# Where weight tiles lie against activations, modulo 512 bytes, in a two-layer encoder

## Chip, core and metric

The kernel runs on one core of a Trainium2 chip. The metric is the time of one execution on the device in microseconds (us); lower is better. Profiles are one execution each, taken by the hardware profiler. Engines are named PE (TensorE's matmuls), PEld (its weight loads), DVE (VectorE), ACT (ScalarE), POOL (GpSimd) and SP (SyncE, whose queue issues most loads).

## What is computed

Two encoder layers over 256 tokens of width 2,048, in float32. Layer 0 mixes tokens by 2-D neighbourhood attention with a position bias (12 heads), layer 1 by grouped-query attention with rotary positions (12 heads, 4 key heads). In both, 4 more heads attend to 256 memory tokens. The sum of all products with weights is what takes the time:

```python
for i in range(DEPTH):                       # 2
    n = rms_norm(h, attn_norm[i])
    z = n @ (a_w_in[j] if i % 2 == 0 else b_w_in[j])   # 2048 x 5120, 2048 x 3072
    ...                                      # attention of the layer's own heads
    km, vm = jnp.split(m @ w_mem_kv[i], 2, axis=-1)
    cross = memory_attention(...)
    h = h + jnp.concatenate([mix, cross], axis=-1) @ w_o[i]
    n = rms_norm(h, mlp_norm[i])
    h = h + jnp.square(jax.nn.relu(n @ w_up[i])) @ w_down[i]   # width 8192
return rms_norm(h, final_norm)
```

## The kernel before

Every weight chunk of 128 x 2048 float32 (1 MB) is loaded by SP, then taken apart into a high part in the reduced float32 format (`hi`, `uh`, `th`, ...; ScalarE, `split`, L301) and the rest as a low part (`lo`, `ul`, `tl`, ...; VectorE, L302). Activations are held in the same two parts. A product is then three matmuls: high x high, high x low, low x high. A half of a chunk is 128 x 1024, 4,096 bytes in each partition.

There are two sorts of product:

- *S products and up products* (`s_products`, L215; `u_products`, L690): the weight tile is the stationary operand, 128 x 128, and the activations (`memT`, `nT`, `hT`) stream past it, 256 columns. They write `ps_s` (memory keys, q and k of layer 0) and `ps_u` (the MLP's up projection).
- *M products and down products* (`m_products`, L202; the function at L804): the activations are stationary and the weights stream, 512 columns. They write `ps_m` and the seven sums `p1` to `p7` of a Strassen-like scheme, in which `a_s` holds the activations' combinations and `bh`, `bl`, `th`, `tl` the weights'.

The attention itself (`sc_ps` and `av`, L352 to L354 and L386 to L388) multiplies activations alone, 256 columns, in the same pattern of three.

The MLP runs as one long row: `up_grains` of a part and `down_grains` of the part before alternate; on TensorE about 48 up products (two halves of a chunk) stand before 21 down products. A list of grains (`run_all`) decides the program's order; loads, splits and products are issued some grains ahead of each other.

Tiles come from pools. A pool places its tiles one behind the other, so the start of a tile follows from the lengths of those before it. At four places the kernel before sets a start by hand: `MOVING_AT` (160 bytes) and `STILL_AT` (64 bytes) shift the used part of a half inside a tile that is 256 bytes longer than its content, and `wide(name, 480)` shifts `nT` by 480 bytes. Since such a tile is 4,352 bytes long, neighbouring buffers of one name differ by 256, modulo 512. The lines in question:

```python
def new_half(kind):
    s = slice(STILL_AT // 4, STILL_AT // 4 + HALF) if kind == "S" else slice(0, HALF)
    return tuple(at.ring.tile([P, HALF + 64], F32R, tag=n, bufs=4, name=n)[:, s] for n in ("hi", "lo"))
```

Of the kernel before, what the change touches and what calls it, by code (L numbers as in the profile page):

```python
# [10 lines left out]
F32 = mybir.dt.float32  # L11
F32R = mybir.dt.float32r
# [5 lines left out]
P = 128  # L18
# [16 lines left out]
HALF = CH // 2  # L35
# [3 lines left out]
STEPS = PK // 2  # L39
GUARD = 3  # L40

MOVING_AT = 160

STILL_AT = 64
MASKED = -1e30


# [27 lines left out]
def encoder_kernel(ctx: ExitStack, tc: tile.TileContext, t: dict, out: bass.AP):  # L75
# [4 lines left out]
    def opened(name, side="left", space=None, bufs=1):  # L80
        kw = {"space": space} if space else {}
        manager = tc.tile_pool(name=name, bufs=bufs, side=side, reuse_waits="tile", **kw)
        pools[name] = manager, manager.__enter__()
        return pools[name][1]
# [14 lines left out]
    def open_sums():  # L99
        at.acc = opened("ps_acc", space=bass.MemoryType.PSUM, bufs=4)  # L100
        at.att = opened("ps_att", space=bass.MemoryType.PSUM, bufs=4)

    def open_ring():
        at.ring = opened("ring")
        at.cat = opened("cat")

    def open_work():
        at.work = opened("work", side="right", bufs=2)
# [36 lines left out]
    def halves_of(w):  # L145

        tiles = {}

        def load():
            tiles["raw"] = loaded(w.src, "U")  # L150

        def prep_early(hf):
            tiles[hf] = half_of_side(tiles["raw"], hf, MOVING_AT)

        def prep(hf):
            if hf == 0:
                tiles["raw"] = at.ring.tile([P, CH], F32, tag="raw", bufs=3, name="raw")
                nc.sync.dma_start(tiles["raw"], w.src)
            tiles[hf] = new_half(w.kind)
            split(*tiles[hf], tiles["raw"][:, hf * HALF : (hf + 1) * HALF])  # L160

        def run(hf):
            if hf == 0:
                w.start(w)
            hi, lo = tiles.pop(hf)
            if w.kind == "S":
                s_products(w, hf * (KT // 2), KT // 2, hi, lo)
            else:
                for i in range(NT):
                    m_products(w, w.first + 2 * hf, 2, i, hi, lo, w.begins and hf == 0, w.last and hf == 1)  # L170

        def after():
            if w.last:
                w.done(w)
            if w.early == "last":
                to_work()

        if w.early:
            return [Grain(lambda: run(0), None, load, None, lambda: prep_early(0), SOON),
                    Grain(lambda: run(1), after, None, None, lambda: prep_early(1), SOON)]  # L180
        return [Grain(lambda: run(0), None, None, None, lambda: prep(0)),
                Grain(lambda: run(1), after, None, None, lambda: prep(1))]

    def new_half(kind):
        s = slice(STILL_AT // 4, STILL_AT // 4 + HALF) if kind == "S" else slice(0, HALF)
        return tuple(at.ring.tile([P, HALF + 64], F32R, tag=n, bufs=4, name=n)[:, s] for n in ("hi", "lo"))

    pin = tc.keep_in_program_order

# [338 lines left out]

    def x_norm(j):
        if j == 0:  # L530
            box["nT"] = wide("nT0", 480)
        for k in (2 * j, 2 * j + 1):
            split_pair(box["nT"], box["xT"][k // 8][:, k % 8, :], G_A0, k)

# [162 lines left out]
            nc.tensor.matmul(ps, hi[:, s], acts[:, k, SEQ:], start=False, stop=False)  # L697
            nc.tensor.matmul(ps, lo[:, s], acts[:, k, :SEQ], start=False, stop=k == KT - 1)  # L698

    def half_of_side(raw, hf, place=0):  # L700
        s = slice(place // 4, place // 4 + HALF)
        tiles = tuple(at.side.tile([P, HALF + 64], F32R, tag=n, bufs=2, name=n)[:, s] for n in ("uh", "ul"))
        box.setdefault("splits", []).append(split(*tiles, raw[:, hf * HALF : (hf + 1) * HALF]))
        return tiles

# [5 lines left out]
    def up_grains(layer, part, m):  # L711
        own = {}

        def load():
            own["raw"] = loaded(t[f"w_up{layer}"][part * PK + m], "U")

        def prep(hf):
            own[hf] = half_of_side(own["raw"], hf)

        def run(hf):  # L720
            if hf == 0:
                if part == 0:
                    own["ps"] = at.acc.tile([P, 512], F32, tag="acc", name="ps_u")[:, :SEQ]
                else:
                    if part == 1 and m == 0:
                        closed("ps_att", "ps_acc")
                        at.sums = opened("ps_sums", space=bass.MemoryType.PSUM)
                        box["ps"] = {}
                    own["ps"] = at.sums.tile([P, 512], F32, tag="up", name="ps_u")[:, :SEQ]
            u_products(own["ps"], hf * (KT // 2), KT // 2, *own.pop(hf))  # L730

        def after():
            if part == 0 and m == 0:
                closed("cat", "ring")
                at.mlp = opened("mlp")
                box["z"] = [at.mlp.tile([P, 4, 512], F32, tag=f"z{q}", name=f"z{q}") for q in range(2)]
                box["z_set"] = set()
            squared(layer, part, m, own["ps"])

        return [Grain(lambda: run(0), None, load, None, lambda: prep(0), SOON),  # L740
                Grain(lambda: run(1), after, None, None, lambda: prep(1), SOON)]
# [25 lines left out]
    def down_grains(layer, part, n, begins, ends):  # L767

        q, j = part % 2 ^ n // STEPS, n % STEPS
        own = {}  # L770

        def load():
            src = t[f"w_pair{layer}"][(part * 2 + q) * STEPS + j]
            own["b"] = at.side.tile([P, 3 * 512], F32, tag="b", bufs=2, name="b")
            nc.sync.dma_start(own["b"], src[:, : 3 * 512])
            own["t"] = at.side.tile([P, 4, 512], F32, tag="T", bufs=2, name="t")
            nc.sync.dma_start(own["t"][:, 0, :], src[:, 3 * 512 :])

        def behind(fn):

            return (lambda: past(fn, box["splits"][-4])) if part == 0 and n < 2 else fn

        def block(k):

            return own["b"][:, k * 512 : (k + 1) * 512]

        def pre():
            s = own["t"]
            nc.vector.tensor_tensor(s[:, 1, :], s[:, 0, :], block(0), op=ALU.add)  # L789
            nc.gpsimd.dma_start(s[:, 0, :], block(1), accum_op=ALU.add)  # L790

        def prep_first():
            own["first"] = tuple(at.mlp.tile([P, 3 * 512], F32R, tag=x, name=x) for x in ("bh", "bl"))
            split(*own["first"], own["b"])

        def prep_second():
            s = own["t"]
            nc.vector.tensor_tensor(s[:, 2, :], s[:, 1, :], block(1), op=ALU.add)
            nc.vector.tensor_tensor(s[:, 3, :], s[:, 2, :], block(2), op=ALU.add)
            own["second"] = tuple(at.mlp.tile([P, CH], F32R, tag=x, name=x) for x in ("th", "tl"))  # L800
            split(*own["second"], s.rearrange("p a b -> p (a b)"))

        def run(which, products):
            hi, lo = own.pop(which)  # L804
            a = box["a", part, j]
            for name, ai, bi in products:
                if begins:
                    box["ps"][name] = at.sums.tile([P, 512], F32, tag=name, name=name)
                ps, s = box["ps"][name], slice(bi * 512, (bi + 1) * 512)
                nc.tensor.matmul(ps, a[:, 0, ai, :], hi[:, s], start=begins, stop=False)  # L810
                nc.tensor.matmul(ps, a[:, 0, ai, :], lo[:, s], start=False, stop=False)  # L811
                nc.tensor.matmul(ps, a[:, 1, ai, :], hi[:, s], start=False, stop=ends)  # L812

        def after(products):
            if ends:
                for name, _, _ in products:
                    taken(q, name)

        def after_second():
            after(SECOND)  # L820
            if ends:
                box["z_set"].add(q)
            if ends and (part, n) in FOLDS:
                folded(q)

        return [Grain(lambda: run("first", FIRST), lambda: after(FIRST), load, behind(pre), behind(prep_first), SOON),
                Grain(lambda: run("second", SECOND), after_second, None, None, behind(prep_second), SOON)]

# [35 lines left out]
    def plain_grains(layer, nb):  # L864
# [8 lines left out]

        def prep(c, hf):
            if c == 0:
                own[c, hf] = half_of_side(own[0], hf, MOVING_AT)
            else:
                own[c, hf] = tuple(at.mlp.tile([P, HALF], F32R, tag="bt"[hf] + x, name=f"{x}_p") for x in "hl")
                split(*own[c, hf], own[1][:, hf * HALF : (hf + 1) * HALF])
# [59 lines left out]
    def down_done(layer, nb):  # L939
        def f(w):  # L940
# [5 lines left out]
                later(1, times_gf, nb)  # L946
                return
            if nb == 0:
                box["nT"] = wide("nT1", 480)
            later(1, transposed, box["nT"], lambda i, k: h[:, i, k * P : (k + 1) * P],  # L950
                  list(range(nb * 4, nb * 4 + 4)), G_A1)
            if nb == 3:
# [278 lines left out]
```

## Time and profile before

| | us |
|---|---|
| median of 3 runs (2051.68 to 2055.82) | 2052.95 |
| span of the profiled execution (its own time is not recorded apart; the median is 2.35 above the span) | 2050.6 |
| TensorE busy, 13,092 matmuls | 2028.0 |
| weight loads busy | 1835.2 |
| VectorE busy | 1657.1 |
| ScalarE busy | 1242.0 |
| GpSimd busy | 120.2 |

Busy time of TensorE is the union of its matmuls, from start to modelled end. Because they are pipelined, a matmul's listed duration is longer than its distance to the next one's start. That distance is read from the timeline, which has one row per matmul with its start.

### The profile page before, as it was taken

What the parts mean: (1) busy time and instruction counts of PE and PEld (TensorE: products, weight loads), DVE (VectorE), ACT (ScalarE), POOL (GpSimd) and SP (SyncE); (2) the same over time, 40 slices, a digit from 0 to 9 for tenths busy, and PEclk for the clock granted to TensorE, in tenths of its full rate; (3) what the DMA queues carried; (4) which work ended last, traced back from release to release, by engine and by line L of the source; (5) the groups of instructions that cost most, each with busy time, mean ns of one, the idle gap of its engine ahead of it and who ended that gap; (6) DMA issues with size and microseconds to landing.
All of it is one profiled execution on the core that took longest, in us unless ns stands there. A gap on an engine that the chain in (4) does not pass through costs nothing.

```text
span 2050.6 us, 32620 instructions
## 1 busy us (share of the span) xinstructions
PE 2028.0 (99%) x13092; PEld 1835.2 (89%) x13092; DVE 1657.1 (81%) x2025; ACT 1242.0 (61%) x1616; POOL 120.2 (6%) x144
## 2 busy tenths in 40 slices
PE   8999999999999999999999999999999999999998
PEld 7899999889999999999988888889999999999996
DVE  6766666558998999989896667657989999999896
ACT  6645454556666666666655557556666666666664
POOL 0000000000000000000000001000000000000000
PEclk9999999999999999999999999999999999999999
DMA  7755555727777777777765554537878787777773
GB/s 280 284 190 180 189 175 178 275 86 224 234 228 232 218 238 230 220 234 226 232 219 204 178 180 144 195 115 224 242 223 237 215 243 220 232 226 228 231 220 134
DMA packets 93431, 433.84 MB, mean 212 GB/s; under 512 B 10464, under 2 KB 12128, under 8 KB 60128
## 3 DMA queue, kind: packets, MB, share of 16 engines
q1 hardware_dynamic: 75888, 399.25, 57.7%
q0 software_dynamic: 16816, 31.46, 8.7%
q8 instruction: 102, 1.67, 0.3%
q10 hardware_dynamic: 576, 1.05, 0.1%
q14 instruction: 49, 0.40, 0.1%
HBM read 398.17 MB, written 4.19 MB: 196 GB/s over the span
## 4 chain that ended last, share of the span: by engine, by line
PE 94%; DVE 3%; DMA 1%; ACT 1%; issue 1%; SPq 0%; POOLq 0%; POOL 0%; DVEq 0%; ACTq 0%
PE ps_u L698 11%; PE ps_u L696 11%; PE ps_u L697 11%; PE p L810 8%; PE p L811 8%; PE p L812 8%; PE ps_m L209 8%; PE ps_m L212 8%; PE ps_m L213 8%; PE ps_s L221 3%; PE ps_s L223 3%; PE ps_s L222 3%; DVE ul L302 1%; PE pt_a L378 1%; DVE tl L302 1%
## 5 line engine op out<-in xcount | busy, mean ns | idle before, releaser
L698 PE MATMUL ps_u<-hT,ul 128*128 128x256 f32 x2048 | 568.1, 278 | 2.4 <-DVE ul L302 2.3
L696 PE MATMUL ps_u<-hT,uh 128*128 128x256 f32 x2048 | 568.0, 277 | 0.1
L697 PE MATMUL ps_u<-hT,uh 128*128 128x256 f32 x2048 | 567.4, 277 | 0.0
L301 ACT ACTIVATE uh<-raw_U 128x1024 fp32r<-128x1024 f32 x278 | 294.6, 1061 | 303.5 <-PE ps_u L697 281.0
L302 DVE TENSOR_TENSOR lo<-raw,hi 128x1024 fp32r<-128x1024 f32 (+1 forms) x224 | 266.3, 1195 | 162.1 <-ACT hi L301 160.0
L698 PEld LDWEIGHTS ps_u<-hT,ul 128*128 128x128 f32 x2048 | 385.5, 188 | 5.2 <-DVE ul L302 4.2
L696 PEld LDWEIGHTS ps_u<-hT,uh 128*128 128x128 f32 x2048 | 384.9, 188 | 5.5 <-ACT uh L301 0.5
L697 PEld LDWEIGHTS ps_u<-hT,uh 128*128 128x128 f32 x2048 | 384.4, 188 | 4.6
L302 DVE TENSOR_TENSOR ul<-raw_U,uh 128x1024 fp32r<-128x1024 f32 x278 | 337.2, 1218 | 37.5 <-ACT uh L301 37.4
L301 ACT ACTIVATE hi<-raw 128x1024 fp32r<-128x1024 f32 (+1 forms) x224 | 231.8, 1040 | 215.9 <-PE ps_m L213 121.1
L301 ACT ACTIVATE th<-t 128x2048 fp32r<-128x2048 f32 x112 | 215.2, 1921 | 125.4 <-PE p L812 111.8
L302 DVE TENSOR_TENSOR tl<-t,th 128x2048 fp32r<-128x2048 f32 x112 | 256.1, 2286 | 26.4 <-ACT th L301 25.8
L302 DVE TENSOR_TENSOR bl<-b,bh 128x1536 fp32r<-128x1536 f32 x112 | 196.0, 1750 | 0.3 <-ACT bh L301 0.2
L811 PE MATMUL p<-tl,a_s 128*128 128x512 f32 x448 | 177.2, 395 | 0.0
L812 PE MATMUL p<-th,a_s 128*128 128x512 f32 x448 | 174.4, 389 | 0.0
L301 ACT ACTIVATE bh<-b 128x1536 fp32r<-128x1536 f32 x112 | 166.2, 1484 | 10.1 <-PE p L812 4.0
L810 PE MATMUL p<-th,a_s 128*128 128x512 f32 x448 | 166.1, 395 | 0.0
L790 POOL DMA_DIRECT2D t<-b x112 | 97.1, 867 | 1166.0 <-DVE t L789 593.6
L811 PE MATMUL p<-bl,a_s 128*128 128x512 f32 x336 | 131.0, 390 | 0.2 <-DVE bl L302 0.2
L812 PE MATMUL p<-bh,a_s 128*128 128x512 f32 x336 | 131.1, 390 | 0.0
L789 DVE TENSOR_TENSOR t<-t,b 128x512 f32<-128x512 f32 x112 | 77.2, 689 | 64.1 <-DMA t<-in_w_pair 52.5
L223 PE MATMUL ps_s<-nT,lo 128*128 128x256 f32 x448 | 124.9, 279 | 0.0
(233 smaller groups left out, 3813.4 us busy)
## 6 DMA issues: line engine op xcount, KB each, us to landing
raw_U<-in_w_up SPq DMA_DIRECT2D x128, 1024.0 KB, 6.6
b<-in_w_pair SPq DMA_DIRECT2D x112, 768.0 KB, 4.5
raw<-in_w_o SPq DMA_DIRECT2D x32, 1024.0 KB, 5.1
t<-in_w_pair SPq DMA_DIRECT2D x112, 256.0 KB, 3.5
t<-b POOLq DMA_DIRECT2D x112, 256.0 KB, 6.8
raw<-in_w_b SPq DMA_DIRECT2D x21, 1024.0 KB, 5.0
raw<-in_w_av SPq DMA_DIRECT2D x12, 1024.0 KB, 5.1
raw<-in_w_aq SPq DMA_DIRECT2D x12, 1024.0 KB, 5.0
```

Of the source, the lines that this page charges most:

```text
L209: first = nc.tensor.matmul(w.ps[i], ah, hi[:, s], start=st, stop=False)
L212: nc.tensor.matmul(w.ps[i], ah, lo[:, s], start=False, stop=False)
L213: nc.tensor.matmul(w.ps[i], al, hi[:, s], start=False, stop=sp)
L223: nc.tensor.matmul(ps, lo[:, s], acts[:, k, :SEQ], start=False, stop=k == KT - 1)
L301: first = nc.scalar.activation(dst_hi, src, AF.Copy)
L302: return first, nc.vector.tensor_tensor(dst_lo, src, dst_hi.bitcast(F32), op=ALU.subtract)
L696: nc.tensor.matmul(ps, hi[:, s], acts[:, k, :SEQ], start=k == 0, stop=False)
L697: nc.tensor.matmul(ps, hi[:, s], acts[:, k, SEQ:], start=False, stop=False)
L698: nc.tensor.matmul(ps, lo[:, s], acts[:, k, :SEQ], start=False, stop=k == KT - 1)
L810: nc.tensor.matmul(ps, a[:, 0, ai, :], hi[:, s], start=begins, stop=False)
L811: nc.tensor.matmul(ps, a[:, 0, ai, :], lo[:, s], start=False, stop=False)
L812: nc.tensor.matmul(ps, a[:, 1, ai, :], hi[:, s], start=False, stop=ends)
```

## The change

The shifts by hand go. Halves become 4,096 bytes long, a multiple of 512, so all buffers of one name start at the same place modulo 512. Small tiles named `apart`, of 32 to 288 bytes, are allocated ahead of the others and never used; they move what follows.

```diff
-MOVING_AT = 160
-STILL_AT = 64
...
+    def apart(pool, size):
+        pool.tile([P, size // 4], F32, tag="apart", bufs=1, name="apart")
     def open_ring():
         at.ring = opened("ring")
+        apart(at.ring, 288)
         at.cat = opened("cat")
+        apart(at.cat, 256)
...
-            tiles[hf] = half_of_side(tiles["raw"], hf, MOVING_AT)
+            tiles[hf] = half_of_side(tiles["raw"], hf)
...
     def new_half(kind):
-        s = slice(STILL_AT // 4, STILL_AT // 4 + HALF) if kind == "S" else slice(0, HALF)
-        return tuple(at.ring.tile([P, HALF + 64], F32R, tag=n, bufs=4, name=n)[:, s] for n in ("hi", "lo"))
+        return tuple(at.ring.tile([P, HALF], F32R, tag=n, bufs=4, name=n) for n in ("hi", "lo"))
...
-            box["nT"] = wide("nT0", 480)
+            box["nT"] = wide("nT0")
...
-    def half_of_side(raw, hf, place=0):
-        s = slice(place // 4, place // 4 + HALF)
-        tiles = tuple(at.side.tile([P, HALF + 64], F32R, tag=n, bufs=2, name=n)[:, s] for n in ("uh", "ul"))
+    def half_of_side(raw, hf):
+        tiles = tuple(at.side.tile([P, HALF], F32R, tag=n, bufs=2, name=n) for n in ("uh", "ul"))
...
                 at.mlp = opened("mlp")
+                at.mlp.tile([P, 8], F32, tag="apart0", bufs=1, name="apart0")
...
+            if part == 0 and n == 0:
+                apart(at.side, 64)
...
         def prep_first():
+            if part == 0 and n == 0:
+                apart(at.mlp, 256)
...
-                own[c, hf] = half_of_side(own[0], hf, MOVING_AT)
+                own[c, hf] = half_of_side(own[0], hf)
...
-                box["nT"] = wide("nT1", 480)
+                box["nT"] = wide("nT1")
```

In the built programs the operands start at these places, in bytes modulo 512. *Distance* is the start of the stationary operand less that of the moving one; a step along a tile changes it by multiples of 512 only. It is taken between a matmul's moving operand and the weights loaded for the next one, which in these rows have the same place as its own.

| products | weights before | activations before | distance before | weights after | activations after | distance after |
|---|---|---|---|---|---|---|
| `ps_s` (stationary `hi`, `lo`; 256 columns) | 192, 448 in turn | 128 | 64, 320 | 416 | 160 | 256 |
| `ps_u` (stationary `uh`, `ul`; 256 columns) | 224, 480 in turn | 160 | 64, 320 | 416 | 160 | 256 |
| `ps_m` (moving `hi`, `lo`; also `uh`, `ul`; 512 columns) | 128, 384 in turn | 128 | 0, 256 | 416 | 160 | 256 |
| `p1` to `p7` (moving `bh`, `bl`, `th`, `tl`; 512 columns) | 128 | 128 | 0 | 416 | 160 | 256 |
| `sc_ps`, `av` (attention; 256 columns) | none | 480 and 480 | 0 | none | 480 and 480 | 0 |

The instructions of PE, ACT, DVE and POOL stand in the same order as before, and so do SP's loads. What a load waits for follows from which tiles overlap older ones. SP's queue at the end of layer 0's MLP, where the first weight chunks of mixer B (`raw`, three buffers in the ring) are loaded, before:

```order
L708 DMA raw_U<-in_w_b 128x2048 [waits DMAHW7_49,DVE_49]
L708 DMA raw_U<-in_w_b 128x2048 [waits DMAHW1_49,DVE_49]
L158 DMA raw<-in_w_b 128x2048 x2
L158 DMA raw<-in_w_b 128x2048 [waits DMAHW6_49]
L158 DMA raw<-in_w_b 128x2048 [waits DMAHW4_49,DVE_49]
```

And the same place of the changed program:

```order
L708 DMA raw_U<-in_w_b 128x2048 [waits DMAHW7_49,DVE_49]
L708 DMA raw_U<-in_w_b 128x2048 [waits DMAHW1_49,DVE_49]
L160 DMA raw<-in_w_b 128x2048
L160 DMA raw<-in_w_b 128x2048 [waits PE_49]
L160 DMA raw<-in_w_b 128x2048 [waits DMAHW6_49]
L160 DMA raw<-in_w_b 128x2048 [waits DMAHW4_49,DVE_49]
```

No load moved; the second of the `raw` loads now waits for a matmul, because the buffer has slid over the first bytes of a tile of the MLP's pool that TensorE still reads. Two `raw_U` loads at the start of layer 0's MLP wait for later matmuls than before for the same reason.

## The prediction

> **What bounds the kernel now.** I read the page first: the span, the engines, the chain.
>
> ```profile
> span 2050.6 us, 32620 instructions
> PE 2028.0 (99%) x13092; PEld 1835.2 (89%) x13092; DVE 1657.1 (81%) x2025; ACT 1242.0 (61%) x1616; POOL 120.2 (6%) x144
> PE 94%; DVE 3%; DMA 1%; ACT 1%; issue 1%; SPq 0%; POOLq 0%; POOL 0%; DVEq 0%; ACTq 0%
> ```
>
> TensorE is busy for 99% of the span and makes 94% of the chain that ended last. So the interval from one matmul's start to the next one's is what counts. The mean duration that the page gives for a matmul is a latency: matmuls overlap, and it hides that interval. Next come the windows of single tiles (stretch, its length, then per engine the busy time and the number of instructions): `ps_u` over the whole run, `ps_s` over its stage, and all work in a stretch of the MLP.
>
> ```profile
> 0.00:2051.00 2051.00, 727.51 (x6144) 722.45 (x6144) 46.84 (x128) 1.00 0.67 212
> 0.00:440.00 440.00, 209.75 (x1728) 204.87 (x1728) 15.01 (x36) 1.00 0.59 209
> 500.00:1080.00 580.00, 579.64 (x3848) 528.55 (x3847) 533.76 (x574) 370.79 (x372) 46.23 (x53) 1.00 0.76 227
> ```
>
> There are 6,144 matmuls of 256 columns into `ps_u` and 1,728 into `ps_s`. In the MLP VectorE is busy for 533.76 of 580 us, so a TensorE that is slower gives it more room, and one that is faster soon meets it. Clock 1.00: no throttle to reckon with.
>
> Now the interval, in the timeline of TensorE (start, duration, line, tiles). First one stretch of 48 up products behind the down products. By the layout its first 24 weight tiles lie 64 bytes, modulo 512, from `hT`, the next 24 (from 813.02) 320 bytes.
>
> ```profile
> 810.26 0.28 PE L696 MATMUL ps_u<-hT,uh 128*128 128x256 f32 x1
> ...
> 810.86 0.28 PE L698 MATMUL ps_u<-hT,ul 128*128 128x256 f32 x1
> ...
> 813.02 0.28 PE L696 MATMUL ps_u<-hT,uh 128*128 128x256 f32 x1
> ...
> 815.74 0.40 PE L810 MATMUL p<-th,a_s 128*128 128x512 f32 x1
> ```
>
> Five intervals take 0.60 us (120 ns each). Then 19 take 2.16 us and 24 take 2.72 us: 113.5 ns, at distance 64 as at 320, with no step where the distance changes. I call this the tight state. Nearly all such stretches look like this one. In nine stretches of 46 the tight state is never reached; here is the first:
>
> ```profile
> 707.20 0.28 PE L698 MATMUL ps_u<-hT,ul 128*128 128x256 f32 x1
> ...
> 712.61 0.39 PE L810 MATMUL p<-th,a_s 128*128 128x512 f32 x1
> ```
>
> 5.41 us for 46 is 117.6 ns, again alike at 64 and at 320: the loose state. So the profile already holds a third kind, which decides my forecast: matmuls of the same form (two on one weight, a third on the low part) whose operands lie at distance 0. These are the attention's, and the longest unbroken row of them is:
>
> ```profile
> 1295.76 0.28 PE L352 MATMUL sc_ps<-kT,qT 128*128 128x256 f32 x1
> 1295.88 0.28 PE L353 MATMUL sc_ps<-kT,qT 128*128 128x256 f32 x1
> ...
> 1297.56 0.39 PE L213 MATMUL ps_m<-hi,cat 128*128 128x512 f32 x1
> ```
>
> Fifteen intervals in 1.80 us: 120.0 ns, and it stays there.
>
> **The change part by part.** *Which distance is the new one like?* No 256-column matmul of the kernel before lies at 256, so its price has to come from elsewhere. The 512-column products do have both: the ring's tiles, 4,352 bytes long, stand in turn 0 and 256 bytes from the activations. Here are two entries into them behind the attention, the first at distance 0, the second at 256:
>
> ```profile
> 1266.12 0.39 PE L209 MATMUL ps_m<-hi,cat 128*128 128x512 f32 x1
> 1266.35 0.40 PE L212 MATMUL ps_m<-lo,cat 128*128 128x512 f32 x1
> 1266.58 0.40 PE L213 MATMUL ps_m<-hi,cat 128*128 128x512 f32 x1
> 1266.82 0.39 PE L209 MATMUL ps_m<-hi,cat 128*128 128x512 f32 x1
> 1267.04 0.39 PE L212 MATMUL ps_m<-lo,cat 128*128 128x512 f32 x1
> ...
> 1268.20 0.39 PE L209 MATMUL ps_m<-hi,cat 128*128 128x512 f32 x1
> ```
>
> ```profile
> 1297.79 0.40 PE L209 MATMUL ps_m<-hi,cat 128*128 128x512 f32 x1
> 1298.02 0.40 PE L212 MATMUL ps_m<-lo,cat 128*128 128x512 f32 x1
> 1298.26 0.39 PE L213 MATMUL ps_m<-hi,cat 128*128 128x512 f32 x1
> 1298.48 0.39 PE L209 MATMUL ps_m<-hi,cat 128*128 128x512 f32 x1
> ...
> 1299.64 0.39 PE L213 MATMUL ps_m<-hi,cat 128*128 128x512 f32 x1
> ```
>
> From 1266.12 the intervals are 0.23, 0.23, 0.24, 0.22; from 1297.56 (its row stands above) they are 0.23, 0.23, 0.24, 0.22 as well, and nine take 2.08 us both times. An irregular pattern that is the same at 0 and at 256, with 64 and 320 alike in the stretch above, speaks for one thing: the hardware sees these distances modulo 256, and 256 is 0. Then the change takes the 256-column products from the good distance to the one that costs 120.0 ns.
>
> *Up products.* 6,144 matmuls are 128 stretches of 48. A usual stretch lasts 810.26 to 815.74, 5.48 us; at 120.0 ns it lasts 5.76, 0.28 more. 128 x 0.28 = 35.8 us. The nine loose stretches gain only 46 x 0.120 - 5.41 = 0.11 each instead of 0.27, so 1.4 less: **+34.4 us**. The distance of every one of them becomes 256, and all lie on the path. From below, the price per matmul is that of the tight state throughout (113.5 ns, the nearest row for "nothing worse than now"): 128 x (48 x 0.1135 - 5.48) = -4 us, and 1.8 us less for the nine. From above it is 120.0 ns; no row has a steady interval above that. I take 120.0, since only the row at distance 0 is like the new one modulo 256.
>
> *`ps_s` products (mixer A's q, k, memory).* 1,728 matmuls, now partly tight, partly loose. At 120.0 each costs 2.4 ns more if it was loose, 6.5 if tight: 4 to 11 us. Most are tight: **+8 us**. From below, all tight: about -2.
>
> *512-column products* (`p1` to `p7`, `ps_m`; 0, or 0 and 256, become 256): by the two entries above **0**. Bounds: nine intervals took 2.08 us, and the tight state would be nine at 2 x 0.1135, 2.04; so an entry without its pattern would save 0.04 us, and with some 150 such entries the most there is to win is 6 us; a loss of as much is the other end.
>
> *Splits on ScalarE and VectorE.* Same instructions, other addresses. Their durations hardly move over the four placements that the kernel before has:
>
> ```profile
> L302 DVE TENSOR_TENSOR ul<-raw_U,uh x278: 1209/1218/1227, 377.6 to 2026.6; 128x1024 fp32r<-128x1024 f32 x139
> ```
>
> (shortest, median, longest, in ns.) 9 ns on 1,218 is nothing beside VectorE's idle 8%: **0**.
>
> *Waits of moved tiles.* Tiles that slide over others make three loads on SP wait for other, later matmuls. The latest of them: the second `raw_U` load of layer 0 waits for the attention's matmul at 341.23, and the second `raw` load of mixer B for the product at 1110.60:
>
> ```profile
> 341.23 0.28 PE L354 MATMUL sc_ps<-kT,qT 128*128 128x256 f32 x1
> 369.28 0.90 SPq L708 DMA_DIRECT2D raw_U<-in_w_up x2
> 1110.60 0.39 PE L213 MATMUL ps_m<-h_p,a_p 128*128 128x512 f32 x1
> 1111.16 1.59 SPq L158 DMA_DIRECT2D raw<-in_w_b x3
> ```
>
> The first matmul ends 28 us before the load is issued, the second ends at 1110.99, just before the group of loads in which the waiting one is second. **0**; if the margin there were lost, the loads behind it on SP would start under 1 us late. The unused tiles are never written: no instruction, **0**.
>
> Sum: 34.4 + 8 = 42.4 us. On the profiled execution that makes 2,093 us of span; its span is 2.3 us below the median of the three runs, 2,052.95, so on the median 2,095 us.
>
> **The rivals.**
> (1) *256 is really the opposite place*: the hardware sees 512 bytes, and at 256 the tight state is always reached. For it: 64 and 320 are both good, so a wide band around 256 might be. Against it: the identical patterns at 0 and 256. It would win the 4 + 1.8 us of the up products and 2 of `ps_s`, perhaps some of the 6 of the 512-column products: 2,039 to 2,046, most likely 2,044. It decides as soon as an up stretch takes under 5.48 us.
> (2) *Placement is immaterial*, and the 120 ns of the attention are due to its short rows. For it: the first five intervals of every up stretch also take 120 ns at distance 64. Against it: those fall to 113 within five, the attention's stay at 120.0 for fifteen. It gives 2,053. This is also the rule of the Trainium skill, "TensorE: Matmul & The Clock Gate", section "Step-by-step: what each phase is for": the engine has two independent read ports, and "Loading the next tile's weights doesn't steal SBUF read bandwidth from the running matmul." By that rule nothing would change, and the time would be 2,053; that 113.5, 117.6 and 120.0 ns stand for one form of matmul is not what it leads one to expect, but the trace alone doesn't prove that a read port is the reason.
> (3) *Never tight, never worse*: all stretches at the loose 117.6. For it: the loose state also lasts for whole stretches. Against it: no row at distance 0 shows it for long. 128 x (48 x 0.1176 - 5.48) = 21 us, and 2 to 4 for `ps_s`: 2,077.
>
> **How the numbers follow.** My forecast, 120.0 for all 256-column products: 0.64, with its own range of 2,086 to 2,100 (`ps_s` 4 to 11, the 512-column products by up to 6 either way). Rival 3: 0.08. Rival 2: 0.11. Rival 1: 0.17. A measurement of this kernel tells about 0.2%, 4 us, from no change: slower 0.72, same 0.11, faster 0.17. To hold 8 in 10, the range leaves out rival 1 and a little at the top: 2,049 to 2,102. The predicted time is that of the likeliest case, 2,095.
>
> **What would show it.** Right: in the timeline of the changed kernel an up stretch of 48 takes 5.76 us with intervals of 0.12 throughout, `ps_u` busy rises from 727.51 by about 34 us and `ps_s` from 209.75 by about 8, while nine 512-column intervals behind the attention still take 2.08. Wrong: intervals of 113 in the middle of an up stretch. Then the period is not 256 bytes, or the attention's 120 has another cause, and the sum falls with its first term. The durations of the splits and the two loads' landing would be unchanged in every case.

## The result, and the profile after

The changed kernel takes 2087.76 us (median of 4 runs, 2087.24 to 2087.97) against 2052.53 for the kernel before in the same comparison: a ratio of 1.0171, with a 95% interval of 1.0158 to 1.0183. It is 1.7% slower. The forecast was 2,095.

The page after, span, engines and chain:

```profile
span 2085.5 us, 32620 instructions
PE 2064.4 (99%) x13092; PEld 1877.3 (90%) x13092; DVE 1665.1 (80%) x2025; ACT 1240.2 (59%) x1616; POOL 119.1 (6%) x144
PE 98%; ACT 1%; DVE 0%; DMA 0%; issue 0%; POOLq 0%; POOL 0%; SPq 0%; ACTq 0%
```

TensorE is 36.4 us longer busy (2028.0 before), with the same 13,092 matmuls. VectorE's share of the chain, 3% before, is 0%: it hardly holds TensorE up any more. The windows of `ps_u` (whole run), of `ps_s` (its stage), and of all work in the same 580 us of the MLP as before; the numbers behind the length are PE, PEld, then DVE:

```profile
0.00:2090.00 2090.00, 759.83 (x6144) 755.30 (x6144) 46.35 (x128) 1.00 0.65 208
0.00:445.00 445.00, 218.18 (x1728) 213.22 (x1728) 15.05 (x36) 1.00 0.58 206
500.00:1080.00 580.00, 580.00 (x3798) 533.50 (x3797) 525.93 (x560) 364.56 (x366) 47.01 (x54) 1.00 0.75 224
```

(In the row of `ps_u` the third engine is ScalarE, which reads it.) `ps_u` grew by 32.3 us and `ps_s` by 8.4. In 580 us TensorE does 3,798 matmuls instead of 3,848, and VectorE's load fell from 533.76 to 525.93 us. The granted clock is 1.00, as before. Now one up stretch and the down stretch behind it, in TensorE's timeline (start, duration, line, tiles):

```profile
837.41 0.28 PE L697 MATMUL ps_u<-hT,uh 128*128 128x256 f32 x1
...
843.16 0.40 PE L815 MATMUL p<-th,a_s 128*128 128x512 f32 x1
...
847.95 0.28 PE L697 MATMUL ps_u<-hT,uh 128*128 128x256 f32 x1
```

48 up products last 5.75 us, where the stretch shown of before lasted 5.48; every interval in it but the first (113) is about 120 ns. The 21 down products behind them last 4.79. In the kernel before, the down stretch that starts at 815.74 ends with this row:

```profile
820.56 0.28 PE L696 MATMUL ps_u<-hT,uh 128*128 128x256 f32 x1
```

That was 4.82 us: the down stretches became 0.03 us *shorter*. The nine 512-column intervals behind the attention did not change; here is the first start and the tenth:

```profile
1287.37 0.40 PE L210 MATMUL ps_m<-hi,cat 128*128 128x512 f32 x1
...
1289.44 0.39 PE L210 MATMUL ps_m<-hi,cat 128*128 128x512 f32 x1
```

To see all of it at once I add up the intervals from each TensorE instruction's start to the next one's, by kind of product, over the whole timeline. An interval that is over 30 ns longer than the tight one (113.3 ns for 256 columns, which the prediction read as 113.5 from rounded rows; 226.7 for 512) is put down as a wait, with what it has above the tight one:

| us | before | after | change | forecast |
|---|---|---|---|---|
| up products (`ps_u`), without waits | 702.8 | 736.1 | +33.3 | +34.4 |
| `ps_s` products, without waits | 198.2 | 206.7 | +8.5 | +8 |
| down products (`p1` to `p7`), without waits | 540.3 | 536.7 | -3.6 | 0 (bounds -6, +6) |
| `ps_m` products, without waits | 502.1 | 502.1 | 0 | 0 |
| waits that begin at an up product | 7.7 | 5.6 | -2.1 | 0 |
| waits that begin at a down product | 0.9 | 0.2 | -0.7 | 0 |
| first to last TensorE start | 2034.4 | 2069.8 | +35.4 | +42.4 |

(The last row also holds the attention, the transposes and the other waits, which agree before and after to 0.1 us a kind.) The two large terms are as forecast; 6.4 of the missing 7 us were given back in two places that it had put at nothing.

### The profile page after: what moved, and what is told of

It reads as the page before. It is cut to its first block, busy times and chain, and to the rows that moved or that the text cites. A ratio compares the mean times of both kernels' runs of the same rounds, so it can differ in the third digit from the quotient of the medians.

```text
span 2085.5 us, 32620 instructions
## 1 busy us (share of the span) xinstructions
PE 2064.4 (99%) x13092; PEld 1877.3 (90%) x13092; DVE 1665.1 (80%) x2025; ACT 1240.2 (59%) x1616; POOL 119.1 (6%) x144
## 4 chain that ended last, share of the span: by engine, by line
PE 98%; ACT 1%; DVE 0%; DMA 0%; issue 0%; POOLq 0%; POOL 0%; SPq 0%; ACTq 0%
PE ps_u L699 12%; PE ps_u L698 12%; PE ps_u L697 12%; PE p L815 9%; PE p L816 9%; PE p L817 9%; PE ps_m L210 8%; PE ps_m L213 8%; PE ps_m L214 8%; PE ps_s L222 3%; PE ps_s L224 3%; PE ps_s L223 3%; PE pt_a L379 1%; PE pt_n L320 1%; PE sc_ps L354 0%; PE sc_ps L355 0%
## 5 line engine op out<-in xcount | busy, mean ns | idle before, releaser
L699 PE MATMUL ps_u<-hT,ul 128*128 128x256 f32 x2048 | 580.0, 283 | 1.5 <-DVE ul L303 1.5
L698 PE MATMUL ps_u<-hT,uh 128*128 128x256 f32 x2048 | 579.5, 283 | 0.0
L697 PE MATMUL ps_u<-hT,uh 128*128 128x256 f32 x2048 | 579.2, 283 | 0.0
L697 PEld LDWEIGHTS ps_u<-hT,uh 128*128 128x128 f32 x2048 | 392.7, 192 | 5.4
L698 PEld LDWEIGHTS ps_u<-hT,uh 128*128 128x128 f32 x2048 | 392.5, 192 | 4.4
L699 PEld LDWEIGHTS ps_u<-hT,ul 128*128 128x128 f32 x2048 | 392.5, 192 | 2.9 <-DVE ul L303 1.9
L303 DVE TENSOR_TENSOR ul<-raw_U,uh 128x1024 fp32r<-128x1024 f32 x278 | 338.5, 1222 | 44.0 <-ACT uh L302 42.1
L222 PE MATMUL ps_s<-nT,hi 128*128 128x256 f32 x448 | 127.0, 284 | 0.0
```

Source lines behind the costliest of these rows:

```text
L222: nc.tensor.matmul(ps, hi[:, s], acts[:, k, :SEQ], start=k == 0, stop=False)
L303: return first, nc.vector.tensor_tensor(dst_lo, src, dst_hi.bitcast(F32), op=ALU.subtract)
L697: nc.tensor.matmul(ps, hi[:, s], acts[:, k, :SEQ], start=k == 0, stop=False)
```

## The experiments

A *place* is here the distance of the prediction modulo 256: start of the stationary operand less that of the moving one. *Entry* is the same distance across a border: the first up weights less the last down weights that streamed. *Way back* is the first `a_s` tile less the `hT` that streamed last. By these definitions entry and way back always add up to the place of the up products plus that of the down products. With both places held, one can't be changed without the other. *Tight*, *loose* and *120* are the three states of the prediction; "48-long" are the stretches of 48 up products that follow a whole down stretch.

### 256 against 0

All distances of the change are moved by 256:

```diff
-        apart(at.ring, 288)
+        apart(at.ring, 32)
-        apart(at.cat, 256)
-                apart(at.side, 64)
+                apart(at.side, 320)
-                apart(at.mlp, 256)
```

> The changed kernel with every weight tile at distance 0 instead of 256, modulo 512, nothing else. Theory (the distance counts modulo 256 bytes, so 256 is 0): the same time as the changed kernel, 2088 us within 4, and up products 120 ns apart in stretches of 5.76 us. Rival (512 bytes count, and 256 is a bad place of its own): the 256-column products differ from 120 ns, with a tight state of 113 ns the time would be near 2050.

2087.49 us (ratio 1.0172, 1.0158 to 1.0186), and the four rows of products agree with those of after within 0.1 us: 736.1, 206.7, 536.7, 502.1. So 256 is 0, and rival 1 is out. It also speaks against another rival, that the start of the weights alone counts: 120 ns stand here with both operands at 160, after with 416 against 160, and in the attention with 480 against 480.

### Up products back at 64, but without buffers in turn

```diff
-                apart(at.side, 64)
+                apart(at.side, 256)
```

The pool `side` ends at a fixed address, and in the built program `uh` and `ul` stand ahead of this unused tile. So a tile that is 192 bytes longer moves them 192 bytes *down*, from 416 to 224, and `b` behind it stays.

> The changed kernel with one number changed: the unused tile ahead of uh and ul is 256 bytes long instead of 64, so the up products alone lie at distance 64, in all buffers alike; ps_s and the 512-column products of the down projection stay at 256. Theory (the distance of the 256-column products is what costs): up stretches of 48 back to about 5.48 us, 33 us less than the changed kernel, 2055 us; ps_s stays at 120 ns. Rival (what costs is that all buffers of a name now start at the same place, where before two places took turns): up products stay at 120 ns and the time at 2088, since the buffers still start alike.

2075.26 us (1.0113, 1.0099 to 1.0126), 20 above the expected time. One of its 48-long stretches:

```profile
771.05 0.28 PE L697 MATMUL ps_u<-hT,uh 128*128 128x256 f32 x1
...
776.71 0.40 PE L815 MATMUL p<-th,a_s 128*128 128x512 f32 x1
```

5.66 us for 48 is 117.8 ns: loose, and so are all the others of 48. The kernel before has the same place of 64 and is tight. The place alone doesn't decide between tight and loose. The rival fell too: the up products left 120 ns, and `ps_u` gave back 13.3 of its 33.3 us (722.8).

### Up and `ps_s` products at 64 and 320 in turn, as before

Only the down products and the way in and out of them stay as the change has them:

```diff
     def new_half(kind):
-        return tuple(at.ring.tile([P, HALF], F32R, tag=n, bufs=4, name=n) for n in ("hi", "lo"))
+        s = slice(16, 16 + HALF) if kind == "S" else slice(0, HALF)
+        return tuple(at.ring.tile([P, HALF + 64], F32R, tag=n, bufs=4, name=n)[:, s] for n in ("hi", "lo"))
...
         def prep(hf):
-            own[hf] = half_of_side(own["raw"], hf)
+            own[hf] = half_of_side(own["raw"], hf, 64)
```

`half_of_side` shifts the used part by its last argument again, as in the kernel before.

> The changed kernel with the up products and the ps_s products at 64 and 320 in turn, as in the kernel before, and the 512-column products of the down projection at 256 as in the changed one (ring and early 512-column products at 0 and 256 in turn). Theory: both 256-column terms go, 33 and 8 us, and what the change won at the entries into the down products (3.6 us) stays: 2044 to 2049 us, under the kernel before (2052.5). Rival (the win at those entries comes from the 120 ns state of the up products ahead of them, not from the placement of the down products): 2050 to 2053.

2065.01 us (1.0064, 1.005 to 1.0077), above both the theory's range and the rival's. `ps_s` falls from 206.7 to 197.7 us and is as before (198.2), with other starts (224 and 480 against 160; before, 192 and 448 against 128) at the same place: that term of the change is the place of `ps_s`. The up products stay loose, 721.5 us, though 64 and 320 now alternate: turns are not what makes them tight. The down products keep what the change won (536.6), now behind loose stretches, so that win doesn't need the 120 ns state ahead of it.

### Up products at sixteen places

On the changed kernel, the up weights go to another place with every chunk, in steps of 16 bytes (64 floats of room in the tiles, so that neighbouring buffers differ by 256):

```diff
+            box["turn"] = box.get("turn", -1) + 1
+            own[hf] = half_of_side(own["raw"], hf, box["turn"] // 2 % 16 * 16)
```

> The changed kernel with the up products' weight tiles at 16 places, 0 to 240 bytes in steps of 16 above their old start, one after the other, each in two buffers that differ by 256: so 32 distances modulo 512 stand in one profile. Theory (period 256 or a divisor of it): the interval of a distance and of that plus 256 agree to 1 ns; 64 and 320 give 113 or 117.6 ns, 0 and 256 give 120. If the period is 128, 128 gives 120 as well. Rival (period 512): distance and distance plus 256 differ at some of the places. Time: between 2055 and 2088, by how wide the good band around 64 is.

2080.02 us (one run). Two stretches, at places 224 and 128:

```profile
731.31 0.28 PE L697 MATMUL ps_u<-hT,uh 128*128 128x256 f32 x1
...
736.91 0.40 PE L817 MATMUL p<-th,a_s 128*128 128x512 f32 x1
```

```profile
836.05 0.29 PE L697 MATMUL ps_u<-hT,uh 128*128 128x256 f32 x1
...
841.82 0.40 PE L817 MATMUL p<-th,a_s 128*128 128x512 f32 x1
```

5.60 and 5.77 us. The down products stay at 0 here, so each place comes with one entry, equal to itself, and a way back of 0. Mean interval in the steady part of a stretch, in ns, by place:

| 0 | 16 | 32 | 48 | 64 | 80 | 96 | 112 | 128 | 144 | 160 | 176 | 192 | 208 | 224 | 240 |
|---|---|---|---|---|---|---|---|---|---|---|---|---|---|---|---|
| 120.0 | 118.3 | 118.4 | 118.3 | 113.4 or 117.8 | 118.6 | 117.3 or 118.9 | 119.6 to 120.1 | 119.9 | 120.0 | 119.8 to 120.1 | 118 | 117.8 | 116.7 | 116.6 | 117.3 |

A distance and the same plus 256 agree within some 0.4 ns (at 16, 118.5 and 118.3; at 144, 119.9 and 120.0), as expected, so the period is 256 over the whole circle. It is not 128: 128 is as dear as 0, but 80 and 208 differ by 2 ns. 64 is the only place of the sixteen with a tight state, and only in the long first row of each layer, where other up products stand ahead of it; behind down products it is loose each time. 112 to 160 are as dear as 0.

### What makes 64 tight: the entry or the down products?

Both kernels start from the one with the up products at 64 throughout. In the first, `a_s` and the down weights move 32 bytes down, so the down products stay at 0, the entry becomes 96 and the way back 224, both as before the change. In the second only the down weights move: the entry is 96 too and the way back stays 0, but the down products lie at 32.

```diff
-                at.mlp.tile([P, 8], F32, tag="apart0", bufs=1, name="apart0")
...
-                apart(at.mlp, 256)
```

```diff
-                apart(at.mlp, 256)
+                apart(at.mlp, 224)
```

> The kernel u64 with the MLP's pool 32 bytes lower and no unused tile ahead of bh: a_s and the down products' weights at 128, as in the kernel before. So the first weights of an up stretch lie 96 bytes from the last down product's moving weights (in u64: 64), and everything else of u64 stays, up products at 64 in all buffers alike. Theory (which of two states a stretch at 64 falls into is set by the distance at its entry, from the product ahead): the stretches return to the tight state, 113 ns, about 20 us less than u64, and the entries into the down products return to the dearer pattern, 3.6 us more: 2059 us. Rival (the tight state needs the two places 64 and 320 that took turns): the stretches stay loose, 117.7 ns, 2075 to 2079.

> The kernel u64 with only the down products' weights 32 bytes lower: a_s stays at 160, so the down products lie at 288 (32 modulo 256), the entry into an up stretch at 96, the entry into the down products stays at 0. Theory (the entry decides): tight up stretches, 20 us less than u64, and the cheaper entries into the down products stay, so 2055 if 512-column products cost nothing extra at 32. Rival: the down products' own distance matters too, and their 2352 matmuls pay for leaving 0 by 1 to 8 ns each, 2 to 20 us: 2057 to 2075.

The first took 2063.5 us (1.0046, 1.0031 to 1.0061, before 2054.01), 4.5 above the theory's time and far below the rival's. The second took 2087.61 (1.0164, 1.0147 to 1.0181), above both of its expectations. An up stretch of the first, then an up and a down stretch of the second:

```profile
735.49 0.28 PE L697 MATMUL ps_u<-hT,uh 128*128 128x256 f32 x1
...
740.97 0.40 PE L814 MATMUL p<-th,a_s 128*128 128x512 f32 x1
```

```profile
773.33 0.28 PE L697 MATMUL ps_u<-hT,uh 128*128 128x256 f32 x1
...
778.98 0.39 PE L815 MATMUL p<-th,a_s 128*128 128x512 f32 x1
...
783.87 0.28 PE L697 MATMUL ps_u<-hT,uh 128*128 128x256 f32 x1
```

In the first, 5.48 us: all 96 stretches of 48 are tight, most of those of 46 loose, as before the change; up products 703.1 us, down products 540.3, both as before. (`ps_s` lies at 0 in both kernels, 206.7 us; that is 8.5 of the 9.5 us by which the first is slower than before.) In the second, 5.65 us: every 48-long stretch loose at the same entry, and the down stretch takes 4.89 instead of 4.79; all down products together 548.1, 11.5 more than at 0. So neither the up place nor the entry decides alone, and the 512-column products have a place that matters too. The two places in turn are not needed: the first kernel is tight without them.

### Down products at sixteen places

Up products at 64, `a_s` as in the change; the down weights (`bh`, `bl` and in the same way `th`, `tl`) move by 16 bytes every seven steps:

```diff
+            box["step"] = box.get("step", -1) + 1
+            own["at"] = box["step"] // 7 % 16 * 4
+            c = slice(own["at"], own["at"] + 3 * 512)
+            own["first"] = tuple(at.mlp.tile([P, 3 * 512 + 64], F32R, tag=x, name=x)[:, c] for x in ("bh", "bl"))
```

> The kernel u64 with the down products' weights moved through 16 places in steps of 16 bytes, seven steps of the MLP at each. It gives for each place the steady interval of the 512-column products and the state of the up stretch (at 64) behind it. Theory: the state of the up stretches changes with the place, tight at an entry of 96 and loose at 64, while their own distance stays. Rival (the state is set by the distance of the up products alone): loose at all 16 places. For the 512-column products I expect 226.7 ns once steady at most places, since they lock at 0 and at 256; if more, by 1 to 8 ns.

2073.8 us (one run). At 0 the last eight intervals of a down stretch are at 226.6 ns; at the other places they are longer, between 227.6 and 236.8 (16: 236.7; 96: 234.1; 192: 228.5). The one exception is the last row of twelve at 144, which runs at 226.6 where those ahead of it at 144 take about 230. I had expected 226.7 at most places: a miss. Here are a down stretch at 0 and one at 16, 4.78 and 4.95 us:

```profile
514.77 0.40 PE L817 MATMUL p<-th,a_s 128*128 128x512 f32 x1
...
519.55 0.28 PE L697 MATMUL ps_u<-hT,uh 128*128 128x256 f32 x1
...
1964.01 0.39 PE L817 MATMUL p<-th,a_s 128*128 128x512 f32 x1
...
1968.96 0.28 PE L697 MATMUL ps_u<-hT,uh 128*128 128x256 f32 x1
```

And the up stretches, all at 64, come out tight or loose by where the down products lie: the 48-long ones are all tight at 64 and 96, for example, and all loose at 128 and 144. The way back is 0 throughout this run, so it doesn't decide alone either. At 112, 208 and 224 they are strictly in turn; first rows of two up and two down stretches at 208:

```profile
727.36 0.28 PE L697 MATMUL ps_u<-hT,uh 128*128 128x256 f32 x1
...
733.02 0.40 PE L817 MATMUL p<-th,a_s 128*128 128x512 f32 x1
...
737.92 0.28 PE L697 MATMUL ps_u<-hT,uh 128*128 128x256 f32 x1
...
743.36 0.39 PE L817 MATMUL p<-th,a_s 128*128 128x512 f32 x1
```

5.66 us, then 5.44, with the same addresses. So the addresses alone don't fix the state here. It goes with what the stretch ahead did: the down stretches take turns as well, 4.83 and 4.90 us.

### Entries at steps of 32 bytes

Down products at 0 again. The `ps_s` products lie at 64 and 320 in turn, as in the run above that has them in turn, and the up products at 64 in all buffers (the unused tile in `side` is 256 bytes long). On top of that `a_s` and the down weights move together, to another place in each layer; the numbers are (16, 24), (32, 40) and (48, 56) in the three kernels:

```diff
-                at.mlp.tile([P, 8], F32, tag="apart0", bufs=1, name="apart0")
+                at.mlp.tile([P, (16, 24)[layer]], F32, tag="apart0", bufs=1, name="apart0")
```

> The kernel of the run us64 (up and ps_s products at 64, down products at 0, modulo 256) with a_s and the down weights moved together, so that the down products stay at 0 and only the entry changes: from the last down weights to the first up weights 32 bytes in layer 0 and 0 in layer 1 (before: 96, and tight; us64: 64, and loose). The way back, from the last up products to the first a_s tile, becomes 32 and 64. Theory A, the entry's distance decides once the down products lie at 0: all 48-long up stretches of one layer are alike, so a layer's up products sum to 351.5 us (tight) or 361 (loose), and the time is 2065 (none tight), 2055.5 (one layer) or 2046 (both), up to 4 more where the entry into the down products costs its 60 ns instead of 28. Theory B, the state is carried over from stretch to stretch and the addresses only bias it: tight and loose stretches mixed within a layer, 2048 to 2063.

> As entry32_0, with the entry into the up products at 224 bytes in layer 0 and 192 in layer 1, modulo 256; the way back 96 and 128. Theory A: each layer uniform, 2065, 2055.5 or 2046, up to 4 more by the entries into the down products. Theory B: mixed within a layer, 2048 to 2063.

> As entry32_0, with the entry into the up products at 160 bytes in layer 0 and 128 in layer 1, modulo 256; the way back 160 and 192. Theory A: each layer uniform, 2065, 2055.5 or 2046, up to 4 more by the entries into the down products. Theory B: mixed within a layer, 2048 to 2063.

2064.6, 2057.59 and 2056.27 us (one run each; before 2053.07), all within theory A's figures. In the second, a 48-long stretch of layer 0 (entry 224) and one of layer 1 (entry 192):

```profile
850.80 0.28 PE L698 MATMUL ps_u<-hT,uh 128*128 128x256 f32 x1
...
856.26 0.39 PE L816 MATMUL p<-th,a_s 128*128 128x512 f32 x1
...
1816.89 0.28 PE L698 MATMUL ps_u<-hT,uh 128*128 128x256 f32 x1
...
1822.55 0.39 PE L816 MATMUL p<-th,a_s 128*128 128x512 f32 x1
```

5.46 against 5.66 us. All 48 such stretches of a layer are alike in each of the three kernels, so with the down products at 0 theory A holds:

| entry | 0 | 32 | 64 | 96 | 128 | 160 | 192 | 224 |
|---|---|---|---|---|---|---|---|---|
| way back | 64 | 32 | 0 | 224 | 192 | 160 | 128 | 96 |
| 48-long up stretches | loose | loose | loose | tight | loose | tight | loose | tight |
| usual down stretch less 21 x 226.7 ns, in ns | -1 | 58 | 26 | 62 | 15 | 50 | -3 | 32 |

(Column 64 is from the first run with the up products at 64, column 96 from the kernel before. The last row is the median, and it depends on the stretch ahead too: in the kernel before it is 62 behind a tight stretch and 25 behind a loose one.) The entry and the way back always add up to 64 here, so these runs don't tell which of the two sets the state.

### A version put together from this

Up and `ps_s` products at 64, down products at 0, the entry at 160 or 224 in both layers:

```diff
-                at.mlp.tile([P, (16, 24)[layer]], F32, tag="apart0", bufs=1, name="apart0")
+                at.mlp.tile([P, (48, 48)[layer]], F32, tag="apart0", bufs=1, name="apart0")
```

With (32, 32) the entry is 224.

> The version put together from the runs: up and ps_s products at 64 modulo 256, down products at 0, the entry into the up products at 160 in both layers. Theory A (with the down products at 0 the entry's distance decides the state): layer 1's 48-long up stretches are tight like layer 0's in entry160_128, both layers' up stretches sum to 308.1 us each and the down products to 269.7, 3.7 us less per layer than before (310.8, 270.7, and 44.5 for the first long row in both): 2045.5, 0.36% faster than before. Theory B (the layer or the history decides, the entry only happened to agree): layer 1 is loose or mixed, 2050 to 2056, no faster than before.

> As both160, with the entry at 224 in both layers. Theory A: both layers like layer 0 of entry224_192, up 308.8 and down 269.6 us each: 2046.5, 0.3% faster than before. Theory B: layer 1 loose or mixed, 2050 to 2056.

| | median of 11 | recorded ratio to before (median 2052.70, 21 runs) | up | down | `ps_s` | `ps_m` |
|---|---|---|---|---|---|---|
| entry 160 | 2049.44 | 0.9982 (0.9973 to 0.999) | 698.5 | 539.3 | 197.3 | 503.8 |
| entry 224 | 2047.90 | 0.9979 (0.997 to 0.9988) | 700.5 | 537.6 | 198.7 | 503.8 |

Both intervals lie below 1: some 0.2% faster than before. The page at entry 224, and a 48-long stretch of layer 1, which was loose at 192:

```profile
span 2045.8 us, 32620 instructions
PE 2023.5 (99%) x13092; PEld 1832.9 (90%) x13092; DVE 1659.0 (81%) x2025; ACT 1243.6 (61%) x1616; POOL 119.2 (6%) x144
PE 97%; DVE 1%; ACT 1%; DMA 0%; issue 0%; SPq 0%; POOLq 0%; POOL 0%; ACTq 0%
```

```profile
1809.69 0.28 PE L698 MATMUL ps_u<-hT,uh 128*128 128x256 f32 x1
...
1815.15 0.39 PE L816 MATMUL p<-th,a_s 128*128 128x512 f32 x1
```

5.46 us: it is the entry (with the way back, which moves with it) and not the layer that decides, and theory B is out. They came 3.9 us (160) and 1.4 us (224) later than expected. For 1.7 us in each that is `ps_m` (503.8 against the 502.1 of the kernel from which the sum was made). The plain products at the end of the MLP stream half of their weights from `uh` and `ul`; these moved with the up products, and no longer lie at 0 against the activations. Those matmuls take 44.8 us instead of 43.6, which is some 1.2 of the 1.7. At entry 160, waits at the down products come to 3.0 us instead of 0.2 at entry 224, and the page's chain has VectorE and a load in it again, as before the change:

```profile
PE 91%; DVE 4%; DMA 2%; issue 1%; ACT 1%; SPq 0%; POOLq 0%; POOL 0%; DVEq 0%; ACTq 0%
```

The longest of these waits is a product that needs VectorE's low part (the brackets name the idle time before it and what ended it):

```profile
867.51 0.50 PE L817 MATMUL p<-tl,a_s 128*128 128x512 f32 x1 [0.64 <-DVE tl L304]
```

At entry 224 the up stretches are as tight, and no such wait stands there. So the tight state alone doesn't make these waits, and why they come at one entry only is not shown.

## Why the prediction was right, and where not

*The interval as the thing to read: right.* Not one instruction was added or moved; the 1.7% are in the distance from one matmul's start to the next.

*256 is 0: right.* The step was taken from two entries of 512-column products that looked alike at 0 and 256. The kernel with all distances at 0 gives the same time to 0.3 us, and the sixteen places agree in pairs 256 apart. At the time the two entries were a weaker sign than the prediction took them for, since no row showed that unequal places give unequal patterns. The sweep of the down products shows it afterwards: 512-column products settle differently at other places.

*Up products, +34.4: measured +33.3*; a stretch 5.75 us for the 5.76 forecast, `ps_u` busy +32.3. The 120.0 ns was the right row. What was only half right is the other end, 113.5 ns as the price of place 64. Moved back to 64 alone, the up products give back 13.3 us; nearly all of the other 20.0 came back in the first kernel with the old entry of 96 and way back of 224 (703.1). The prediction saw both states in its rows and didn't ask what chooses between them. Its sum didn't need it, since all stretches end at 120 ns.

*`ps_s`, +8: measured +8.5*; moved back to 64 and 320, it gives back 9.0.

*512-column products, 0 (bounds 6 either way): the mis-sized term, -3.6.* The settled interval didn't change, which was right; the entry did. In the kernel before, a down stretch lasts 4.82 us behind a tight up stretch and 4.79 behind a loose one. The latter starts at 712.61, the last row of the prediction's second stretch, and ends with this row:

```profile
717.40 0.28 PE L696 MATMUL ps_u<-hT,uh 128*128 128x256 f32 x1
```

After, all 94 stretches of 21 last 4.79. The term was bounded from the entries behind the attention, which stayed as they were; the entries behind the up products, which are nearly all of them in the MLP, were not looked at one by one. The first kernel with entry 96 has the 540.3 back, but it has the tight up stretches back too. Since the kernel before shows both lengths at the same addresses, the state of the stretch ahead can account for the 3.6 us; the way back has a share in it as well, by the last row of the table of entries, and the runs don't part the two.

*Waits, 0: -2.8.* The prediction said in its first part that a slower TensorE gives VectorE room, and then gave this no term. The page's waits of `ps_u` on VectorE fall from 2.3 to 1.5 us. Six intervals of the MLP's rows that held waits of 0.2 to 0.46 us before (the two longest at 484 and 1415 us, in the first long row of up products of each layer; 2.1 us in all) hold less than 0.2 after, and VectorE is gone from the chain (3% to 0%). These 2.8 and the 3.6 above are most of the 7 us by which the sum, 42.4, was above the 35.4 measured.

*Splits and unused tiles, 0: right.* The row of the same split after:

```profile
L303 DVE TENSOR_TENSOR ul<-raw_U,uh x278: 1215/1222/1230, 385.6 to 2061.5; 128x1024 fp32r<-128x1024 f32 x139
```

1,222 ns for 1,218. *Moved loads, 0: right as far as it shows*: `ps_m` has 502.1 us and 5.1 us of waits in both kernels.

*Rivals.* (1) fell with the kernel at 0. (2), placement immaterial, fell with the change itself: 736.1 against 702.8 us for the same 6,144 matmuls. By the rule of the Trainium skill, "TensorE: Matmul & The Clock Gate", section "Step-by-step: what each phase is for", that loading the next weights takes no read bandwidth from the running matmul, this difference should not be there; the measurement decides, but these runs don't show that the reads are what meets. (3), never tight and never worse, is not what happens at 0; but the up products do just that at place 64 with an entry of 64: 117.8 ns and 722.8 us, 20.0 above before, where the prediction gave 21.

What stays open: what it is in the chip that repeats every 256 bytes; and what sets the state at place 64. Entry 96 was seen tight and loose, and so was a way back of 0. With the down products at 0 the pair of them settles it, and which of the two counts can't be told, since they add up to a fixed sum.

## What to carry to other kernels

Where TensorE is the bound, read its start-to-start interval stretch by stretch: the listed duration (276 to 283 ns for most up products here) hides steps of 113.3, 117.8 and 120.0 ns that are worth 6%. If one form of matmul shows several steady intervals, tabulate the operands' starts modulo 256 bytes before looking for another cause, and try the place of the stretch ahead as well as the stretch's own. A slower bound gives its neighbours room, so a sum of pure losses is too high: give that a term.

## What was not expected of the hardware

- The dear places are not only 0: from 112 to 160 modulo 256 a 256-column product takes 119.5 to 120.2 ns, and around 208 to 224 it takes 116.6. The kernel's own place, 64, is the only one of sixteen at which 113.3 ns occurred at all; the others were seen with one entry each behind the down products.
- At that place two states are stable for whole stretches, 113.3 and 117.8 ns, with the same addresses; at some places of the down products they take turns from one stretch to the next.
- The 512-column products of the MLP settle at 226.7 ns at place 0; elsewhere it is 227.6 to 236.8, but for one row of twelve at 144. So the best place of one form (64) is not that of the other (0).
